# Ten slots instead of eight for the prepared expert weights of a decoder trunk, and two loads fewer ahead

## The chip, the cores and the metric

One core of a Trainium2 chip runs the whole program. The metric is the device time in microseconds. Before the change it is 1417.46 us, the median of three runs (1416.42 to 1417.75).

## The reference

Two decoder layers work on 256 tokens of 1024 features. Each mixes the tokens (a pooling group and a convolution group), norms, and then applies a channel mixer: layer 0 a dense SwiGLU, layer 1 the top 2 of 8 experts. Nearly all weights are the experts':

```python
def moe_swiglu(h, w_router, w1, w3, w2):
    ...
    for e in range(N_EXPERTS):
        out = out + gates[:, e:e + 1] * swiglu(t, w1[e], w3[e], w2[e])
```

w1 and w3 are 1024 x 3584, w2 is 3584 x 1024, all float32.

## The kernel before, in words

**Heads and rests.** TensorE multiplies in fp32r, which keeps fewer bits than float32. So each weight is split: ScalarE casts it to fp32r (the head, `nc.scalar.copy` in `Weights.advance`, L146) and VectorE subtracts the head from it (the rest, `Weights.rest`, L161). `mm` then issues three matmuls for each 128 rows of weights: activations' head by weights' head (L347), head by rest (L351), activations' rest by weights' head (L352). Where the activations' head and rest stand side by side in one tile, two do: L347 and L349.

**The experts.** The tokens of an expert are gathered into a tile of 128 places. Experts at even places of `SEQ` are *wide*: 128 places for tokens, three matmuls. Those at odd places are *narrow*: 64 places, heads beside rests, two matmuls, and a shift that folds the halves (L1052). An expert is cut into seven chunks of 512 hidden features. `BLOCKS` lists the 56 chunks: four wide ones first, then narrow and wide ones by turns, and four narrow ones last. Below, a *pair* is a narrow chunk with the wide one after it. `experts` runs over them: w1 of this chunk, w3 of this chunk, then w2 of the chunk before (`both`, `both`, `down`); SiLU is on ScalarE (L652), the gated product on VectorE (`glu`, L661), and `hidden` turns that product by four transposes on TensorE (L335) and splits it (L320 and L321, narrow: L381 and L382). Where the next expert is due, gather (L796) and scatter (L814, L815) lie in between.

**Items and slots.** Each chunk has six *items* of 128 x 2048 (1 MB): two of w1, two of w3, two of w2. All items lie in a pool of 19 slots of that size (`SLOTS`). An expert item takes three slots in its life: the loaded float32 one (SyncE, L117), a head and a rest. The loaded slot is free after the rest is made, head and rest after TensorE's last matmul on them. `get(i)` calls `advance`, which prepares items in order as long as those prepared and not yet used take at most `hl` slots, and keeps `ahead()` loads before the next item to prepare:

```python
            full = not it["direct"] and self.live(False) + it["slots"] > self.hl
...
        return max(1, SLOTS - self.temps - self.hl - self.live(True))
```

While the experts run, `hl` is `HL_MOE` (set in `moe` once the first chunk's w3 is done), and `temps` is 1, from the last seven chunks on 4. Engines run their instructions in the order in which they are emitted; a tile that finds no free slot waits for one to come free, so which slot it gets is settled when the program is built.

**Near the end** (`MORE_AT`, chunk 53) all engines read a count and branch (L1038, L1039).

Of the kernel before, what the change touches and what calls it, by code (L numbers as in the profile page):

```python
# [33 lines left out]
DENSE_CHUNKS = [(c * 512, min(512, DFF - c * 512)) for c in range((DFF + 511) // 512)]  # L34
ND = len(DENSE_CHUNKS)
SLOTS = 19
HL_START, HL_PRE, HL_FIRST, HL_SECOND, HL_MOE = 8, 12, 8, 6, 8
WO0 = 0
DIRECT = ("pw0", "pw1", "wo00", "wo01")
DT = ((20, 21), (20, 21))  # L40
# [1269 lines left out]
```

## Time and profile before

| what | value |
| --- | --- |
| median of three runs | 1417.46 us |
| the profiled execution's own time | 1417.34 us |
| its span | 1415.6 us |
| TensorE (PE) busy | 1310.6 us, 93% |
| VectorE (DVE) busy | 1199.9 us, 85% |
| ScalarE (ACT) busy | 938.9 us, 66% |
| moved by DMA | 433.07 MB, mean 306 GB/s |
| expert loads | 336 of 1 MB, median 8.0 us to landing |

The profile is that of one execution. Its span is 1.7 us shorter than its own time. The experts fill the stretch from about 490 to 1370 us. A matmul's duration there (some 0.39 us) includes its way through the array and overlaps with the next, so a busy TensorE is not one at its peak: what a wait costs is read from the distance of two starts.

### The profile page before, as it was taken

What the parts mean: (1) busy time and instruction counts of PE and PEld (TensorE: products, weight loads), DVE (VectorE), ACT (ScalarE), POOL (GpSimd) and SP (SyncE); (2) the same over time, 40 slices, a digit from 0 to 9 for tenths busy, and PEclk for the clock granted to TensorE, in tenths of its full rate; (3) what the DMA queues carried; (4) which work ended last, traced back from release to release, by engine and by line L of the source; (5) the groups of instructions that cost most, each with busy time, mean ns of one, the idle gap of its engine ahead of it and who ended that gap; (6) DMA issues with size and microseconds to landing.
All of it is one profiled execution on the core that took longest, in us unless ns stands there. A gap on an engine that the chain in (4) does not pass through costs nothing. (4 is left out here: it accounts for less than half of the span.)

```text
span 1415.6 us, 16882 instructions
## 1 busy us (share of the span) xinstructions
PE 1310.6 (93%) x6186; PEld 1060.0 (75%) x6186; DVE 1199.9 (85%) x1082; ACT 938.9 (66%) x883; POOL 92.3 (7%) x71
## 2 busy tenths in 40 slices
PE   6769999999869999999999999999999999999877
PEld 5638888888637887777777778778777777778656
DVE  3996844557966889999999999999999999999885
ACT  4543634426533668887887787787787788788662
POOL 0430000010560200000000000000000000000000
PEclk8889999999988999999999999999999999999999
DMA  9335755427544589999999999999999999999950
GB/s 381 121 119 178 266 180 179 178 97 272 196 173 177 204 334 406 420 387 350 418 417 354 402 420 353 391 417 367 384 421 376 375 409 387 371 360 423 356 191 30
DMA packets 62170, 433.07 MB, mean 306 GB/s; under 512 B 6960, under 2 KB 7472, under 8 KB 11008
## 3 DMA queue, kind: packets, MB, share of 16 engines
q1 hardware_dynamic: 60336, 425.60, 77.0%
q0 software_dynamic: 1168, 4.23, 0.9%
q10 hardware_dynamic: 576, 2.10, 0.5%
q8 instruction: 50, 0.82, 0.2%
q14 instruction: 40, 0.33, 0.1%
HBM read 430.85 MB, written 1.05 MB: 305 GB/s over the span
## 5 line engine op out<-in xcount | busy, mean ns | idle before, releaser
L161 DVE TENSOR_TENSOR w<-w 128x2048 fp32r<-128x2048 f32 (+1 forms) x460 | 895.9, 1988 | 72.6 <-ACT w L146 61.7
L146 ACT CAST w<-w 128x2048 fp32r<-128x2048 f32 (+1 forms) x460 | 751.1, 1671 | 157.1 <-PE p L351 39.5
L347 PE MATMUL p<-w,xH 128*128 128x512 f32 (+1 forms) x1096 | 434.5, 396 | 8.8 <-DVEq L1039 5.8
L352 PE MATMUL p<-w,xL 128*128 128x512 f32 (+1 forms) x648 | 251.0, 387 | 1.3 <-DVE xL L321 1.3
L351 PE MATMUL p<-w,xH 128*128 128x512 f32 (+1 forms) x648 | 250.3, 386 | 0.4 <-DVE w L161 0.4
L347 PEld LDWEIGHTS p<-w,xH 128*128 128x128 f32 x1096 | 207.8, 190 | 50.3 <-issue 6.5
L349 PE MATMUL p<-w,xH 128*128 128x512 f32 x448 | 180.3, 402 | 16.6 <-DVE w L161 16.6
L347 PE MATMUL y<-w,gH 128*128 128x512 f32 x448 | 176.4, 394 | 1.8 <-DVE gH L382 1.6
L352 PEld LDWEIGHTS p<-w,xL 128*128 128x128 f32 x648 | 122.5, 189 | 26.7 <-DVE xL L321 1.8
L351 PEld LDWEIGHTS p<-w,xH 128*128 128x128 f32 x648 | 122.7, 189 | 24.8 <-DVE w L161 1.3
L349 PEld LDWEIGHTS p<-w,xH 128*128 128x128 f32 x448 | 85.0, 190 | 46.8 <-DVE w L161 30.7
L347 PEld LDWEIGHTS y<-w,gH 128*128 128x128 f32 x448 | 84.6, 189 | 21.0 <-DVE gH L382 2.7
L490 DVE SCALAR_TENSOR_TENSOR yc<-w,vec,yc 128x256 f32<-128x256 f32 x156 | 91.8, 661 | 0.0
L349 PE MATMUL y<-w,gH 128*128 128x512 f32 x224 | 88.4, 395 | 2.4 <-DVE w L161 2.4
L351 PE MATMUL y<-w,gH 128*128 128x512 f32 x224 | 89.7, 400 | 0.0
L352 PE MATMUL y<-w,gL 128*128 128x512 f32 x224 | 87.4, 390 | 0.0
L498 POOL TENSOR_TENSOR gH<-gH,w 128x512 f32<-128x512 f32 x38 | 66.3, 1744 | 107.9 <-ACT w L495 105.5
L429 POOL DMA_DIRECT2D w<-in_pT x2 | 1.2, 580 | 984.6 <-DVE w L161 826.2
L652 ACT ACTIVATE s<-p 128x512 f32<-128x512 f32 (+1 forms) x69 | 41.0, 596 | 28.5 <-PE p L352 28.5
L321 DVE TENSOR_TENSOR gL<-tr,gH 128x512 fp32r<-128x512 f32 x38 | 25.6, 684 | 32.6 <-ACT gH L320 32.6
L351 PEld LDWEIGHTS y<-w,gH 128*128 128x128 f32 x224 | 42.0, 188 | 14.1 <-DVE w L161 6.0
L349 PEld LDWEIGHTS y<-w,gH 128*128 128x128 f32 x224 | 42.6, 190 | 11.7 <-DVE w L161 3.0
(223 smaller groups left out, 1454.2 us busy)
## 6 DMA issues: line engine op xcount, KB each, us to landing
w<-in_exp_w SPq DMA_DIRECT2D x336, 1024.0 KB, 8.0
w<-in_dense_w SPq DMA_DIRECT2D x33, 1024.0 KB, 5.1
w<-in_w_out SPq DMA_DIRECT2D x8, 1024.0 KB, 6.5
w<-in_ple_gate_w SPq DMA_DIRECT2D x8, 1024.0 KB, 5.3
w<-in_w_gv SPq DMA_DIRECT2D x6, 1024.0 KB, 6.1
w<-in_w_u SPq DMA_DIRECT2D x4, 1024.0 KB, 9.6
w<-in_w_gv SPq DMA_DIRECT2D x4, 512.0 KB, 6.9
w<-in_w_small SPq DMA_DIRECT2D x2, 1024.0 KB, 10.2
```

The lines of the kernel that those rows point to most:

```text
L146: nc.scalar.copy(h, w)
L161: engine.tensor_tensor(l, w, h.bitcast(F32), op=ALU.subtract)
L321: nc.vector.tensor_sub(dst.l, src, dst.h.bitcast(F32))
L347: nc.tensor.matmul(ps, x.h, wh, start=start, stop=False)
L349: nc.tensor.matmul(ps, x.h, wl, start=False, stop=stop)
L351: nc.tensor.matmul(ps, x.h, wl, start=False, stop=False)
L352: nc.tensor.matmul(ps, x.l, wh, start=False, stop=stop)
L429: nc.gpsimd.dma_start(pT.f, a["pT"][l])
L490: nc.vector.scalar_tensor_tensor(yc[:, ct], src, w1, yc[:, ct], op0=ALU.mult, op1=ALU.add)
L498: nc.gpsimd.tensor_tensor(part[b], part[b], p, op=ALU.add)
L652: nc.scalar.activation(s_[:, :nf], p1[:, :nf], AF.Silu)
```

## The change

`HL_MOE`, the number of slots for heads and rests while the experts run, goes from 8 to 10: five items instead of four. By `ahead()` the loads ahead go from 19 - 1 - 8 = 10 to 19 - 1 - 10 = 8, and in the last seven chunks (`temps` 4) from 7 to 5.

```diff
-HL_START, HL_PRE, HL_FIRST, HL_SECOND, HL_MOE = 8, 12, 8, 6, 8
+HL_START, HL_PRE, HL_FIRST, HL_SECOND, HL_MOE = 8, 12, 8, 6, 10
```

No instruction is added or taken away. VectorE's order, at the end of w3 of the second wide chunk and the w2 after it; `w_3151`, `w_3255`, `w_3263`, `w_3331`, `w_3333` and `w_3498` are loaded items in the order of their use, `g0` is the gated product, `gL0` the rest of its transposed form. Before:

```order
L161 TENSOR_TENSOR w_3617<-w_3151,w_3616 128x2048
L661 SCALAR_TENSOR_TENSOR g0_3632<-p3_3593,gsl0_3438,s0_3591 128x512
L161 TENSOR_TENSOR w_3637<-w_3255,w_3636 128x2048
L161 TENSOR_TENSOR w_3655<-w_3263,w_3654 128x2048
L321 TENSOR_TENSOR gL0_3671<-tr_3672,gH0_3670 128x512
L161 TENSOR_TENSOR w_3693<-w_3331,w_3692 128x2048
```

The same place with the change:

```order
L161 TENSOR_TENSOR w_3601<-w_3151,w_3600 128x2048
L161 TENSOR_TENSOR w_3619<-w_3255,w_3618 128x2048
L661 SCALAR_TENSOR_TENSOR g0_3634<-p3_3597,gsl0_3438,s0_3595 128x512
L161 TENSOR_TENSOR w_3639<-w_3263,w_3638 128x2048
L161 TENSOR_TENSOR w_3657<-w_3331,w_3656 128x2048
L321 TENSOR_TENSOR gL0_3673<-tr_3674,gH0_3672 128x512
```

The rest of `w_3255` now stands ahead of the gated product, and that of `w_3331` ahead of `gL0`: each rest is one item earlier against the work on activations. ScalarE's order a little further on, around the cast `gH0` of that transposed product. Before:

```order
L146 CAST w_3654<-w_3263 128x2048
L320 CAST gH0_3670<-tr_3672 128x512
L146 CAST w_3692<-w_3331 128x2048
L146 CAST w_3710<-w_3333 128x2048
L652 ACTIVATE s0_3726<-p1_3679 128x512
```

The same place with the change:

```order
L146 CAST w_3638<-w_3263 128x2048
L146 CAST w_3656<-w_3331 128x2048
L320 CAST gH0_3672<-tr_3674 128x512
L146 CAST w_3684<-w_3333 128x2048
L146 CAST w_3712<-w_3498 128x2048
L652 ACTIVATE s0_3728<-p1_3681 128x512
```

The cast of `w_3331` now stands ahead of `gH0` and that of `w_3498` ahead of SiLU: heads, too, are one item earlier. On SyncE the order of the loads stays; one load that stood ahead of the branch of L1039 now stands behind it.

The built programs also tell which earlier tile had a tile's slot. Of 280 expert items in the middle (the 31st load to the 310th), 263 take one slot of head or rest at least from an item three before, which TensorE must have used; with the change 258 take it from one four before. Of the loads, 187 take the slot of the load twelve before, once its rest is made; with the change 162 take that of the load ten before. (The others take a head's or a rest's slot.) So in the program as built, loads held more slots than `ahead()` counts and prepared items fewer than `hl` allows: three items, now four.

## Rows read from the trace of the kernel before

**Rows 1.** The page: slices of the span (DMA share, GB/s).
```profile
PEclk8889999999988999999999999999999999999999
DMA  9335755427544589999999999999999999999950
GB/s 381 121 119 178 266 180 179 178 97 272 196 173 177 204 334 406 420 387 350 418 417 354 402 420 353 391 417 367 384 421 376 375 409 387 371 360 423 356 191 30
```
**Rows 2.** Busy time of each engine in two stretches, experts and end.
```profile
core 0: us, PE busy (x) PEld busy (x) DVE busy (x) ACT busy (x) POOL busy (x), PEclk, DMA share, GB/s
560.00:1300.00 740.00, 715.72 (x3280) 576.59 (x3279) 704.89 (x462) 595.89 (x447) 0.00 (x0) 1.00 0.98 390
1300.00:1400.00 100.00, 80.75 (x327) 60.58 (x326) 86.30 (x76) 64.33 (x64) 4.51 (x5) 0.93 0.60 236
```
**Rows 3.** The same by pair of chunks, seven pairs (the pattern then repeats).
```profile
577.20:607.50 30.30, 29.61 (x132) 23.42 (x131) 29.20 (x18) 25.18 (x19) 0.00 (x0) 1.00 1.01 419
...
641.10:676.20 35.10, 33.38 (x150) 26.89 (x149) 32.58 (x24) 25.51 (x20) 0.00 (x0) 1.00 0.97 362
676.20:706.40 30.20, 29.51 (x132) 23.33 (x131) 29.13 (x18) 25.11 (x19) 0.00 (x0) 1.00 1.01 417
...
sum 225.90, PE 218.17 PEld 175.74 DVE 214.49 ACT 180.73 POOL 0.00; mean PE 31.17 PEld 25.11 DVE 30.64 ACT 25.82 POOL 0.00
```
**Rows 4.** Waits from 560 to 1300 us: total us, times, longest us.
```profile
ACT w L146 <- PE p L351: 34.2, 32, 1.7
...
DVE w L161 <- ACT w L146: 28.3, 59, 1.9
ACT w L146 <- PE y L347: 21.9, 16, 1.9
...
PE p L349 <- DVE w L161: 15.9, 20, 1.7
...
PE ps_xg L796 <- DVE cc L765: 3.5, 3, 1.2
PE tr L335 <- DVE g L661: 3.4, 3, 1.1
```
**Rows 5.** Timeline: w3 of a narrow chunk.
```profile
692.35 4.49 DVE L161 TENSOR_TENSOR w<-w 128x2048 fp32r<-128x2048 f32 x2
...
693.38 0.39 PE L349 MATMUL p<-w,xH 128*128 128x512 f32 x1
693.61 0.39 PE L347 MATMUL p<-w,xH 128*128 128x512 f32 x1
...
694.68 0.50 PE L349 MATMUL p<-w,xH 128*128 128x512 f32 x1 [0.69 <-DVE w L161]
```
**Rows 6.** Costly groups of VectorE and ScalarE, 577.2 to 803.1 us, each form apart.
```profile
L161 DVE TENSOR_TENSOR w<-w 128x2048 fp32r<-128x2048 f32 x85 | 191.7, 2288 | 11.8 <-ACT w L146 9.8 <-DMA w<-in_exp_w 0.9 <-PE y L351 0.4
L661 DVE SCALAR_TENSOR_TENSOR g<-p,gsl,s 128x512 f32<-128x512 f32 x15 | 11.2, 745 | 0.0
...
L146 ACT CAST w<-w 128x2048 fp32r<-128x2048 f32 x85 | 160.6, 1914 | 36.2 <-PE p L351 12.6 <-PE p L347 7.1 <-PE y L347 7.0
```
**Rows 7.** Expert loads issued by 703.9 us and their time to landing around it.
```profile
L117 SPq DMA_DIRECT2D w<-in_exp_w x102: 327/333/384, 363.4 to 703.8; - x102
...
DMA to landing us min/median/max: 6.9/8.4/9.7
```
**Rows 8.** Rests up to 706.3 us, casts up to 729.8 us.
```profile
L161 DVE TENSOR_TENSOR w<-w 128x2048 fp32r<-128x2048 f32 x85 | 192.9, 2299 | 15.0 <-ACT w L146 11.6 <-PE y L351 1.7 <-DMA w<-in_exp_w 0.9
...
L146 ACT CAST w<-w 128x2048 fp32r<-128x2048 f32 x96 | 181.4, 1914 | 42.1 <-PE p L351 15.1 <-PE p L347 6.9 <-PE y L351 6.8
```
**Rows 9.** The end: loads by 1303.9 us, landing there, casts up to 1321.4 us.
```profile
L117 SPq DMA_DIRECT2D w<-in_exp_w x325: 327/333/1278, 363.4 to 1303.7; - x163
...
DMA to landing us min/median/max: 7.0/9.6/11.5
...
L146 ACT CAST w<-w 128x2048 fp32r<-128x2048 f32 x319 | 601.8, 1914 | 124.9 <-PE p L351 38.7 <-PE y L347 23.4 <-PE y L351 22.7
```
**Rows 10.** Timeline: w2 of a narrow chunk, then the wide chunk's transposes.
```profile
713.84 0.39 PE L347 MATMUL y<-w,gH 128*128 128x512 f32 x1
...
716.82 0.74 DVE L661 SCALAR_TENSOR_TENSOR g<-p,gsl,s 128x512 f32<-128x512 f32 x1
...
717.62 0.66 PE L335 MATMUL tr<-con,g 128*128 128x128 f32 x4
```

## The prediction, made before the changed kernel ran

> **What bounds the kernel now.** I read the slices first, for the place of the experts [rows 1]; the reader is to see a DMA share of 9 tenths from the middle on, at 334 to 423 GB/s. Then the engines' busy time there [rows 2]: from 560 to 1300 us TensorE is busy for 715.7 of 740 us at a full clock, VectorE for 704.9, and the DMA share is 0.98. No engine is alone at its bound; each has 2 to 5% left, so a gain can only come from waits of one on another. By pairs of chunks [rows 3] the quickest take 30.2 to 30.3 us, those with a gather or a scatter 33 to 35, and seven pairs make the pattern of 225.9 us. VectorE idles for 225.9 - 214.5 = 11.4 us of them.
>
> Then the waits [rows 4]. TensorE waits 20 times, 15.9 us, for a rest, always at L349: the second matmul of a narrow item, whose head is there and whose rest is not. VectorE waits 59 times, 28.3 us, for a head, and ScalarE, before its casts, for TensorE (34.2 and 21.9 us are the two largest of such rows): it has the loaded item and no slot to put the head in. So the chain is a ring: TensorE frees slots, ScalarE casts, VectorE subtracts, TensorE uses the item. Last, the loads: 102 were issued by 703.9 us [rows 7]; six of them are the first chunk's, so the 102nd is the 96th cast, and that starts only at 729.8 us [rows 8]. Landing took 9.7 us at most there, so the item lay ready for some 16 us. Loads are early and slots for heads and rests are short.
>
> Why it happens in narrow chunks. TensorE's matmuls start 0.23 us apart (693.38 to 693.61) [rows 5]: a narrow item has 8 (1.8 us), a wide one 12 (2.7 us). A rest takes 2.29 us, two in a row 4.49 [rows 5, 6]. So VectorE falls behind by 0.4 us with each narrow item and could gain as much with each wide one, but there it stands waiting for heads, which wait for slots. What it fails to gain in the six wide items is missing in the six narrow ones.
>
> **The change, part by part.**
>
> *One more prepared item.* A head and rest had to wait for TensorE's end of the item three before, now of that four before (the slots of the built program, in the section on the change). Each becomes free to start one item's use earlier: 1.8 us by a narrow item, 2.7 by a wide one. What is it worth? One TensorE wait: the shown one has 694.68 - 693.61 = 1.07 us between two starts, less the usual 0.23, so 0.84 us lost where the row says 0.69; 0.15 us of each wait is hidden in the matmul's own duration [rows 5]. For 20 waits: 15.9 + 20 x 0.15 = 18.9 us [rows 4]. Can all of it go? An earlier start by 1.8 us or more covers 0.84, and the longest wait (1.7 + 0.15 = 1.85) about. But VectorE must find the time: in the pair of the shown wait it idles 30.20 - 29.13 = 1.07 us, more than 0.84; in the pair with the longest, 35.10 - 32.58 = 2.5 us, more than 1.85 [rows 3]. Of its idle time in seven pairs 9.8 us end with a head [rows 6], against some 18.9 x 225.9 / 740 = 5.8 us of TensorE's waits there. So all 18.9 us can go, with VectorE at 97 to 99% afterwards. **-18.9 us.**
>
> *Casts and rests ahead of the gated product.* One rest more stands ahead of `glu` on VectorE, and one cast more ahead of SiLU and of `gH0` on ScalarE. Behind the gated product TensorE's transposes wait: in the shown wide chunk w2 begins at 713.84, the product ends at 717.56, the transposes start at 717.62 [rows 10], so w2's 16 matmuls (3.6 us) just cover it. If VectorE has really run ahead, the extra rest was made in time that was idle before, and nothing is late. If it has not, the product is late by part of a rest, and TensorE stands. Bounds: below, nothing (or even the three waits that stand there now go, 3.4 + 3 x 0.15 = 3.9 us [rows 4]); above, a whole rest, 2.29 us, in each of the 740 / 32.3 = 23 wide chunks, 53 us. I take a value near the lower end, because VectorE's idle time of 9.8 us per seven pairs exceeds what it has to make up: as much again as the three waits of today. **+3.9 us.**
>
> *Two loads fewer ahead.* The load's slot now comes from the load ten before instead of twelve. Two items are 2 x 30.25 / 12 = 5 us, off a margin of 16 in the middle: nothing. At the end the margin is least: the 325th load is issued at 1303.7, is the 319th cast, and that starts at 1321.4; landing took at most 11.5 us, which leaves 6.2 us [rows 9]. Less 5 us about 1 us is left, and a shorter queue lands sooner, too. **0 us**, with a bound of +4: the margin's lack, paid once, since later loads come at the same pace. Below, nothing: an early load cannot gain. The one load now behind the branch would be needed some 15 us later there; no cost.
>
> The sum: -18.9 + 3.9 + 0 = -15.0 us. The profiled execution's own time is 1417.34 us, 0.12 below the median of the runs, so 1402.3 against it, and **1402.4 us** as a median.
>
> **A rule weighed.** At its best slice DMA moved 423 GB/s [rows 1], that is 2.48 us for 1.05 MB, 29.75 us for a pair's twelve. The quick pairs, at 30.2 us and a share of 1.01 [rows 3], can by that row shrink by 0.5 us and not by 0.84. But over seven pairs 84 loads take 208 us of 225.9, and the margin of 16 - 5 = 11 us lends what two quick pairs in a row lack, so the sum keeps the full term.
> The Trainium skill (DMA: Bandwidth & Descriptors, Specifications) gives 358 GB/s as the limit of one core's share of HBM and 435 as that of the fabric. The trace disagrees with the first as a bound here (423 in a slice); by it twelve loads would take 35.1 us and no pair could become quicker, so the sum would be 0. By the second they take 28.9 us (an estimate from that page), and the sum would stay at -15.0.
>
> **The rivals.**
>
> *Loads become the bound.* Each quick pair stops at 29.75 us. For: a share of 1.01 in them. Against: the margin. Three of seven pairs are quick, 10 in 740 us; each keeps 0.84 - 0.5 = 0.34 us of its loss: 3.4 us. Time: 1402.4 + 3.4 = 1406. It lies inside the range.
>
> *The wait only moves.* TensorE no longer waits at L349, but at the transposes for the gated product; or the slots gained by heads and rests do not let VectorE run ahead, because ScalarE, in order, sits at another wait. For: VectorE is busy for 29.1 of 30.2 us in quick pairs already. Against: 59 waits of VectorE for heads. Time: -3 to +2 us, 1414.5 to 1419.5, say 1417. This is also what comes if the program does not do what the change says.
>
> *Slower: the gated product late in every wide chunk.* If cast and rest of the item ahead of it both start only after TensorE's w3, the product ends 1.91 + 2.29 + 0.75 = 4.95 us after it [rows 6], and w2's 16 narrow matmuls cover 3.6: 1.3 us lost, which is just what the three waits of today show (3.9 / 3). In all 23 wide chunks that is 30 us, less the 3.9 there now and the 18.9 gained: +7, 1425 us. It decides from 18 such chunks on. Against: three in 740 us have it now, though three items are ahead and not four.
>
> **How the numbers follow.** Forecast, with the load-bound rival inside it: 0.82, 1392 to 1413. The wait only moves: 0.11, 1413 to 1420. Late product: 0.07, 1420 and above. The lower end of the forecast takes all 18.9 us and the waits at the transposes and at the gather (L765: 3.5 + 0.45) with them: 1417.46 - 18.9 - 3.9 - 3.9 = 1391; I end at 1393. The upper keeps half of the waits and adds the product's and the loads' bound partly: -9.5 + 3.9 + 2 = -3.6, 1413.8; I end at 1413. What lies outside 1393 to 1413 are the two other rivals and a little of the forecast's own ends, 2 in 10. A measurement of this kernel tells about 0.2%, 2.8 us, from no change: faster means under 1414.6, slower over 1420.3. Faster 0.83, same 0.10, slower 0.07.
>
> **What would show it.** Right: from 560 us on, the row of TensorE's waits at L349 falls from 20 to a few; VectorE's waits for heads fall from 28.3 us to under 12; the quick pairs come to 29.3 to 29.8 us; VectorE is busy for 97% or more and GB/s rises from 390 to near 400; the time from load to cast shrinks by 5 us and ScalarE has no new wait for a load. Wrong: the waits at L335 for the gated product grow past 10 us, the pairs stay at 30.2, or after 1290 us casts wait for loads.

## The result and the profile after

The changed kernel takes **1395.68 us** (median of four runs, 1394.91 to 1396.02) against 1417.28 us (1416.42 to 1417.75) of the kernel before on the same chip: a ratio of 0.9842, 95% interval 0.983 to 0.9854. That is 21.6 us faster; forecast were 15.0, with a range of 1393 to 1413. The profiled execution's own time is 1394.91 us, its span 1393.1 us.

The page's slices, which answer to [rows 1]:

```profile
PEclk8889999999989899999999999999999999999998
DMA  9334755526545399999999999999999999999850
GB/s 381 129 112 166 264 187 196 192 69 242 219 167 187 109 363 364 421 421 376 403 420 408 400 421 387 390 421 405 400 421 404 376 420 414 388 378 420 353 211 30
```

The two stages by engine [rows 2]:

```profile
560.00:1300.00 740.00, 728.01 (x3384) 599.23 (x3383) 724.48 (x476) 618.89 (x468) 0.62 (x1) 1.00 1.00 405
1300.00:1400.00 100.00, 71.78 (x306) 56.57 (x304) 65.85 (x70) 42.15 (x48) 3.90 (x4) 0.88 0.41 159
```

In the same 740 us TensorE starts 3384 matmuls instead of 3280, VectorE is busy for 724.5 us instead of 704.9, and loads move 405 GB/s instead of 390. The same seven pairs of chunks as in [rows 3], cut where the same rests end:

```profile
576.60:605.50 28.90, 28.90 (x132) 23.66 (x131) 28.89 (x18) 24.95 (x18) 0.00 (x0) 1.00 1.01 420
...
638.00:672.80 34.80, 34.77 (x158) 28.56 (x157) 32.47 (x24) 27.14 (x22) 0.00 (x0) 1.00 0.97 365
672.80:701.50 28.70, 28.25 (x129) 22.83 (x127) 28.70 (x18) 24.77 (x18) 0.00 (x0) 1.00 1.01 422
...
sum 217.40, PE 214.17 PEld 176.44 DVE 212.53 ACT 180.25 POOL 0.00; mean PE 30.60 PEld 25.21 DVE 30.36 ACT 25.75 POOL 0.00
```

The quick pairs fell from 30.2 to 28.7 and 28.9 us, the seven from 225.9 to 217.4. VectorE's idle time in them went from 11.4 to 4.9 us. The waits from 560 to 1300 us [rows 4] tell why:

```profile
ACT w L146 <- PE p L351: 38.1, 37, 1.7
...
DVE w L161 <- ACT w L146: 13.3, 13, 1.9
...
PEld tr L335 <- DVE g L661: 12.7, 17, 1.6
...
PE tr L335 <- DVE g L661: 5.6, 7, 1.1
...
PE ps_xg L796 <- DVE cc L765: 3.5, 3, 1.2
```

The row of TensorE's waits at L349 is gone: 20 waits, 15.9 us before, none now. VectorE's waits for heads fell from 59 to 13. The waits for the gated product went from 3 to 7.

Where does the gain arise? TensorE's transposes of the gated product of the 49th expert chunk, before and after:

```profile
1256.30 0.60 PE L335 MATMUL tr<-con,g 128*128 128x128 f32 x4
```
```profile
1233.76 0.60 PE L335 MATMUL tr<-con,g 128*128 128x128 f32 x4
```

They start 22.5 us earlier, and the span is 22.5 us shorter: the gain is made up to there and kept. (Rests seem to gain more, the 289th of a whole item 24.8 us, since with the change they run one item further ahead of TensorE. So progress is compared here by TensorE's instructions, not by rests.)

### The profile page after: what moved, and what is told of

Read it like the earlier page. It is cut to its first block, busy times and chain, and to the rows that moved or that the text cites. A ratio compares the mean times of both kernels' runs of the same rounds, so it can differ in the third digit from the quotient of the medians.

```text
span 1393.1 us, 16896 instructions
## 1 busy us (share of the span) xinstructions
PE 1302.4 (93%) x6186; PEld 1067.9 (77%) x6186; DVE 1194.2 (86%) x1082; ACT 936.8 (67%) x883; POOL 92.1 (7%) x71
## 5 line engine op out<-in xcount | busy, mean ns | idle before, releaser
L349 PE MATMUL p<-w,xH 128*128 128x512 f32 x448 | 176.1, 393 | 0.0
L347 PEld LDWEIGHTS y<-w,gH 128*128 128x128 f32 x448 | 84.6, 189 | 21.4 <-DVE gH L382 3.0
L349 PEld LDWEIGHTS p<-w,xH 128*128 128x128 f32 x448 | 85.1, 190 | 17.0
L349 PE MATMUL y<-w,gH 128*128 128x512 f32 x224 | 88.3, 394 | 1.9 <-DVE w L161 1.9
L320 ACT CAST gH<-tr 128x512 fp32r<-128x512 f32 x38 | 21.8, 586 | 43.6 <-PE tr L335 43.0
L349 PEld LDWEIGHTS y<-w,gH 128*128 128x128 f32 x224 | 42.5, 190 | 11.0 <-DVE w L161 2.3
```

The costliest lines, as they stand in the source:

```text
L320: nc.scalar.copy(dst.h, src)
L347: nc.tensor.matmul(ps, x.h, wh, start=start, stop=False)
L349: nc.tensor.matmul(ps, x.h, wl, start=False, stop=stop)
```

## The experiments

**Each part of the change alone.** The theory: slots that waiting loads held do the work once heads and rests have them, not the count `HL_MOE` as such. The rival: the count, which lets preparation run further ahead, does it. Two loads fewer, with the old count:

```diff
-HL_START, HL_PRE, HL_FIRST, HL_SECOND, HL_MOE = 8, 12, 8, 6, 10
+HL_START, HL_PRE, HL_FIRST, HL_SECOND, HL_MOE = 8, 12, 8, 6, 8
...
-        return max(1, SLOTS - self.temps - self.hl - self.live(True))
+        return max(1, SLOTS - self.temps - self.hl - self.live(True) - 2 * self.fewer)
```

(`fewer` is 1 while the experts run.)

> HL_MOE stays 8 (four items counted, casts and rests at their old places in ScalarE's and VectorE's order), but two loads fewer are kept ahead. In the built program loads then hold ten to eleven slots and heads and rests take those of four items before. Theory (slots that loads gave up are the gain): nearly the whole gain, 1394 to 1400 us, no waits of TensorE at L349 for a rest between 560 and 1270 us, and fewer than today's seven waits for the gated product, since it stands one rest earlier. Rival (the count of prepared items, that is the order, is the gain): 1415 to 1420 us, twenty waits at L349 as before.

Measured: 1395.17 us, ratio 0.9835 (0.9814 to 0.9855), as with the whole change. In its program 267 of 280 items take a slot from four items before. Its waits from 560 to 1270 us (its lines are one higher than the change's):

```profile
DVE w L162 <- ACT w L147: 13.9, 29, 1.3
PEld p L350 <- DVE w L162: 8.3, 20, 0.9
PEld y L352 <- DVE w L162: 5.8, 20, 0.3
PE p L350 <- DVE w L162: 1.6, 3, 0.5
```

No wait for a gated product is left here; three small ones for a rest are. So the two loads fewer alone give the whole gain.

Then the count alone, with ten loads ahead as before:

```diff
-        return max(1, SLOTS - self.temps - self.hl - self.live(True))
+        return max(1, SLOTS - self.temps - self.hl - self.live(True) + 2 * self.fewer)
```

> HL_MOE 10 as in the change, but ten loads are kept ahead as before, on the same 19 slots. In the built program loads hold twelve to thirteen slots and 183 of 280 items take a slot of three before. Theory (slots): no gain or a loss, 1412 to 1425 us, the waits at L349 still there, and more waits for the gated product than in the changed kernel. Rival (order): 1394 to 1400 us.

Measured: 1435.09 us, ratio 1.0134 (1.0112 to 1.0156): 17.9 us slower than the kernel before. In its program 183 of 280 items still take a slot from three items before. Its busy time and waits from 560 to 1270 us:

```profile
560.00:1270.00 710.00, 668.76 (x3088) 542.99 (x3087) 665.11 (x437) 560.76 (x421) 0.00 (x0) 1.00 0.98 384
```
```profile
ACT w L147 <- DVE w L162: 45.6, 84, 1.4
DVE w L162 <- ACT w L147: 34.7, 65, 1.7
PE tr L336 <- DVE g L662: 28.7, 28, 1.4
```

This is the mechanism of the slower rival of the prediction: the gated product is late 28 times, 28.7 us, for up to 1.4 us each (the rival's price was 1.3). It is late in most wide chunks, as the rival had it, and in most narrow ones as well, which the rival left out. The rest that was put ahead of it waits for its head, the head for a slot, and the product behind them in VectorE's order waits, too.

**More and fewer items.** Twelve slots and six loads ahead, by the table alone (`HL_MOE` 12):

> HL_MOE 12: six items counted, six loads ahead, five items before in the built program, loads on the slot of eight before. Theory: nothing left to gain in the middle (no rest waits are left), so the pairs from 576 to 1230 us stay within 0.3 us; near the end the margin from landing to cast, 0.7 us in the changed kernel, goes below zero, casts wait for loads after some 1250 us and cost 2 to 8 us: 1397 to 1404 us. Rival (depth still limits): 1385 to 1393 us.

Measured: 1397.55 us, ratio 0.9871 (0.9847 to 0.9895). The theory held: TensorE begins the transposes of the 49th chunk at 1233.7 us, as with the change, so the middle gains nothing, and the span is 2.5 us longer; at the end a cast starts the moment its load lands (margin 0.0 us). And six slots with twelve loads ahead (`HL_MOE` 6):

> HL_MOE 6: three items counted, twelve loads ahead; in the built program 240 of 280 items take a slot of two before, most heads that of a load, so a rest (2.29 us) starts at the end of the item two before and TensorE has one item to cover it. Theory (slots): a narrow item covers 1.8 us, 0.5 us short, and the gated product, behind such a rest, comes late as well: 3 to 5 us a pair, 1480 to 1540 us. Rival (the loads ahead are worth as much as the slots): 1417 us or less, since loads lie ready earlier than ever.

Measured: 1451.15 us, ratio 1.0227 (1.0201 to 1.0253). The direction held, the size was too high, and no transposes wait for a late gated product here, against the theory. In the program 240 of 280 items take a slot from two before, and the waits at L349, which the change took away, grow (560 to 1270 us):

```profile
PEld p L349 <- DVE w L161: 56.8, 73, 2.3
ACT w L146 <- DVE w L161: 53.3, 108, 1.1
DVE w L161 <- ACT w L146: 34.4, 45, 1.4
PE p L349 <- DVE w L161: 24.3, 35, 1.9
```

Twelve slots in the middle and fewer at the end would be better, if the end alone spoiled them: `HL_MOE` 12, and from the last seven chunks on 8 with two loads fewer than the count allows (five).

```diff
-                W.temps = TEMPS_END
+                W.temps, W.hl, W.fewer = TEMPS_END, 8, 1
```

> Six items counted (12 slots) until the last seven chunks, then four, with five loads ahead: the middle of the run with HL_MOE 12 and an end like that of the run with fewer loads alone. Theory: the middle's end (rest of the 289th item) at about 1228 us as with 12, the end without casts that wait for loads: 1391 to 1395 us, a little under the changed kernel. Rival (the depth at the end matters too): 1396 to 1400 us.

Measured: 1396.71 us, ratio 0.9855 (0.9838 to 0.9871). The rival was right. The margin at the end is 2.6 us, and still nothing is gained: from the first expert chunk's transposes to those of the 49th chunk it takes 753.6 us, as with twelve slots throughout, and from there to the end of the span 161.7, where the change takes 159.4. What delays the end is not shown.

**What binds after the change.** VectorE is busy for 97.9% and TensorE for 98.4% of the stage. The change without the in-loop additions of the scattered expert outputs (`tensor_add` in `scatter`, left out in 28 instructions, so the output lacks them):

```diff
-                nc.vector.tensor_add(yo, yo, ps)
+                if add:
+                    nc.vector.tensor_add(yo, yo, ps)
```

> The changed kernel without VectorE's 28 additions of the scattered results (L817) of the first seven experts; the additions are left out, the matmuls before them stay. 28 x 0.61 us = 17 us less for VectorE. Theory A (VectorE, busy for 98% of the stretch, is the bound now): 1378 to 1384 us. Theory B (TensorE at its pace, or the loads at 2.48 us each, bound it as much): a third of it or less, 1390 to 1396 us.

And the change with a quarter of one rest in six made twice:

```diff
+                    if self.made in self.twice:
+                        self.rest(nc.vector, l[:, :512], w[:, :512], h[:, :512])
```

> The changed kernel with a quarter of one rest in six made twice on VectorE (the first w2 item of 55 chunks, 512 columns, the same values again): 55 x 0.58 us = 32 us more. Theory A: the whole of it, 1424 to 1430 us. Theory B (there is slack beside it): 1400 to 1415 us.

Measured: 1386.16 us without the additions (ratio 0.9788, 0.9769 to 0.9807), 1418.15 us with the doubled quarters (1.0006, 0.9996 to 1.0015). The busy time of the first, then of the second:

```profile
560.00:1250.00 690.00, 683.04 (x3188) 563.81 (x3187) 665.48 (x425) 577.04 (x437) 0.00 (x0) 1.00 1.00 406
```
```profile
560.00:1300.00 740.00, 713.09 (x3295) 581.30 (x3294) 731.28 (x509) 601.16 (x449) 0.00 (x0) 1.00 0.98 393
```

Some 19 us less of VectorE's work (28 x 677 ns) give 9.5 us, but between the first and the 49th chunk, where 24 of the 28 additions stood, only 4.3; some 38 us more (55 x 692 ns) cost 22.5, 20.3 of them there. Both times lie between the theories: work that is added counts for some 0.6 of itself, work that is taken away for half or less. In the first run VectorE has idle time (665.5 of 690) and TensorE little (683.0), so the amount of VectorE's work is not all that holds the changed kernel.

**Work taken off VectorE.** One rest in twelve goes to GpSimd, on top of the twelve-slot version (1396.71 us):

```diff
+    for e, c in BLOCKS[:-WIDE_FIRST]:
+        if e % 2:
+            W.slow.add(W.names[f"w2e{e}_{c}"][0])
```

> The kernel above with one rest in twelve (the first w2 item of 24 narrow chunks, used after four wide items) on GpSimd, idle so far. 24 x 2.24 = 54 us less for VectorE. Theory A without contention: a rest of 128x2048 takes some 7 us on GpSimd by the 1.74 us of 128x512 there, ready in time five items ahead: VectorE no longer bounds, loads at 2.48 us do: 1365 to 1380 us. Rival (both engines read SBUF through one port and block each other): 24 x up to 7 us lost on VectorE, 1400 to 1540 us.

Measured: 1424.22 us, ratio 1.0045 (1.0028 to 1.0062), 27.5 us slower than without it. The timeline of one such rest, and VectorE's groups from 560 to 1300 us:

```profile
707.95 5.00 POOL L162 TENSOR_TENSOR w<-w 128x2048 fp32r<-128x2048 f32 x1 [25.23 <-ACT w L147]
...
710.88 4.24 DVE L162 TENSOR_TENSOR w<-w 128x2048 fp32r<-128x2048 f32 x1 [1.73 <-ACT w L147]
```
```profile
L162 DVE TENSOR_TENSOR w<-w 128x2048 fp32r<-128x2048 f32 x254 | 601.8, 2416 | 43.1 <-ACT w L147 35.2 <-POOL w L162 4.4 <-issue 2.4
...
L772 DVE TENSOR_SCALAR m<-con,cc 128x128 f32<-128x128 f32 x12 | 14.0, 1165 | 0.0
```

The rest on VectorE that overlaps it takes 4.24 us: it ends at 715.12, which is GpSimd's end (712.95) plus 2.17, about a whole rest. So it is held until GpSimd is through. The Trainium skill (SBUF — State Buffer, SBUF: two separate sides) says that GpSimd and an instruction of VectorE with two SBUF inputs share a pair of ports, which one of them holds for its whole length. The trace agrees with that for these rests. What it costs shows at TensorE: from 560 to 1270 us it waits 13 times, 15.0 us, for the gated product, which VectorE makes between its rests; without rests on GpSimd it did so 3 times, 1.2 us.

**Fewer loads still.** Since the loads' slots did the work, how few loads are enough? Count 10 as in the change, and three loads ahead until the last seven chunks:

```diff
-        return max(1, SLOTS - self.temps - self.hl - self.live(True))
+        return max(1, SLOTS - self.temps - self.hl - self.live(True) - 5 * self.fewer)
```

> HL_MOE 10 with three loads ahead instead of eight until the last seven chunks; the slots stand there unused or go to heads and rests, which take those of six before; loads take those of eight before (slots) or six. Theory: the margin from landing to cast, 11 us in the middle of the changed kernel, shrinks by 2 to 4 items of 2.6 us, to 1 to 6 us, and the loads' 2.48 us each begin to hold the quick pairs (28.7 us in the changed kernel) near 29.8: 1398 to 1410 us. Rival (loads have room left): 1393 to 1397 us.

Measured: 1392.35 us, ratio 0.9806 (0.9781 to 0.9832). My theory was wrong; the rival was nearer, and the time is below even its bounds. The median time from landing to cast is 0.4 us (10.9 in the change), and ScalarE waits for loads; but TensorE has no wait for a rest (560 to 1270 us):

```profile
ACT w L147 <- DMA w<-in_exp_w: 40.0, 76, 2.0
...
PE ps_xg L797 <- DVE cc L766: 4.5, 3, 2.1
PEld tr L336 <- DVE g L662: 2.6, 6, 0.6
```

The slots come from six items back, so a cast that is late by up to 2.0 us is made up before TensorE wants its item. Then five loads ahead (`- 3 * self.fewer`), with the one of three and the change once more on the same chip:

> Five loads ahead instead of eight until the last seven chunks, everything else as changed. By the theory that any slot taken from loads that wait helps as long as TensorE finds its item, the heads and rests come from about five to six items before, the landing-to-cast margin falls to some 4 us in the middle, and the time lies between the change's 1395.7 and the 1392.4 of three loads ahead: 1391 to 1396. Rival: past four items nothing more is gained and the 3 us between the change and three loads ahead are what different jobs differ by; then all three kernels of this job lie within 2 us of each other.

> Three loads ahead until the last seven chunks, beside the change itself on one chip. If a shorter queue of loads is truly better, it is 2 to 4 us under the change again; by the rival, within 2 us of it.

> The change itself once more, for the comparison on one chip: 1394.5 to 1396.5.

Measured, with 1418.1 us for the kernel before: five loads **1383.29 us** (1382.68 to 1384.87), ratio 0.9761 (0.9745 to 0.9777); three loads 1391.51, ratio 0.9818 (0.9802 to 0.9834); the change 1395.03, ratio 0.9836 (0.9819 to 0.9852). The last two came as expected; the first lies some 8 us below the lower end of what the theory gave. Five loads ahead beat both kernels: 34.8 us under the one before, 11.7 under the change. Its pairs, and its waits from 560 to 1300 us:

```profile
573.90:602.60 28.70, 28.70 (x131) 23.70 (x131) 28.70 (x17) 24.89 (x19) 0.00 (x0) 1.00 1.02 421
602.60:633.30 30.70, 30.45 (x156) 25.59 (x155) 30.70 (x26) 24.55 (x20) 0.00 (x0) 1.00 1.01 420
...
sum 214.70, PE 213.97 PEld 177.44 DVE 211.79 ACT 178.43 POOL 0.00; mean PE 30.57 PEld 25.35 DVE 30.26 ACT 25.49 POOL 0.00
```
```profile
ACT gH L382 <- PE tr L336: 37.8, 23, 2.7
...
DVE w L162 <- ACT w L147: 7.6, 6, 1.3
...
PE ps_xg L797 <- DVE cc L766: 1.2, 3, 0.5
...
PE tr L336 <- DVE g L662: 0.7, 1, 0.7
```

TensorE is busy for 214.0 of 214.7 us; until 1200 us it waits for no rest and no gated product, and ScalarE now waits for TensorE's transposes. That is what the change left on the table: its seven pairs take 217.4, with TensorE waiting for the gated product. The next bound is TensorE's own work, as the table below shows.

**What the series says together.** Two numbers describe each kernel: how many items the order of instructions runs ahead (`HL_MOE` / 2), and how many items back the slot of a head or rest was last used (read from the built program). Two more are read from the traces: the time between the transposes of the first and of the 49th expert chunk, and what TensorE loses in it (of each distance of two starts over 0.25 us, all beyond the usual 0.23).

| order ahead | loads ahead | slots from | us | 1st to 49th chunk | of it lost | what is late |
| --- | --- | --- | --- | --- | --- | --- |
| 3 | 12 | 2 before | 1451.2 | 805.6 | 71.0 | rests |
| 4 | 10 | 3 before | 1417.3 | 776.3 | 41.8 | rests (kernel before) |
| 5 | 10 | 3 before | 1435.1 | 792.2 | 58.2 | gated product |
| 4 | 8 | 4 before | 1395.2 | 749.0 | 15.6 | rests, by little |
| 5 | 8 | 4 before | 1395.7 | 752.8 | 19.9 | gated product, by little (the change) |
| 6 | 6 | 5 before | 1397.6 | 753.6 | 20.5 | gated product, by little; loads at the end |
| 5 | 5 | 5 before | 1383.3 | 742.4 | 10.4 | no rest, no product until 1200 us |
| 5 | 3 | 6 before | 1392.4, 1391.5 | 748.5, 747.0 | 15.6, 14.1 | loads |

Without what is lost, each of these kernels takes 732 to 735 us for the stretch: that is TensorE's own work, and the eight differ by how long TensorE waits. More slots help until loads are late. An order that runs further ahead than the slots brings nothing (1395.2 and 1395.7) or does harm (1417.3 and 1435.1), since the product stands behind a rest that waits. The rows of 5 and 6 ahead with slots from 5 before fit that (1383.3 and 1397.6): in their programs loads, too, mostly take the slot of the same load, eight before. But they also differ in the loads ahead, and the order by itself at five slots was not tried.

## Why the prediction was right, and where its sum was off

**The ring was the bound, and rests were what TensorE missed: right.** The row at L349 fell from 20 to none, VectorE's waits for heads from 28.3 to 13.3 us (forecast: under 12, a little too much), VectorE's share came to 97.9% and GB/s to 405. The two parts run alone show that it is the slots: 1395.17 with the loads' slots alone.

**The term of -18.9 us: right for what it counted, and too small for what it stood for.** The distances of all TensorE starts, from 546 us to the same matmul (1240 us before, 1217 after), hold 38.9 us over the usual ones before and 17.1 after. Of the difference of 21.8 us, 17.7 are the 18 waits for a rest in that stretch, at 0.65 to some 1.9 each, twelve of them at the 0.84 that the prediction read. Another 5.9 are small delays of 0.1 us that no row of TensorE's waits names. In the timeline of before, at the wait of [rows 5] and at the w2 item behind it:

```profile
694.79 0.19 PEld L347 LDWEIGHTS p<-w,xH 128*128 128x128 f32 x1
695.02 0.40 PE L347 MATMUL p<-w,xH 128*128 128x512 f32 x1
...
696.88 0.19 PEld L351 LDWEIGHTS y<-w,gH 128*128 128x128 f32 x1 [0.30 <-DVE w L161]
696.88 0.50 PE L351 MATMUL y<-w,gH 128*128 128x512 f32 x1
...
697.22 0.39 PE L352 MATMUL y<-w,gL 128*128 128x512 f32 x1
```

The matmul behind the wait starts 0.34 us after 694.68, not 0.23: 0.10 more per wait. And at 696.88 only the weight load waited, 0.30 us; TensorE has no wait there, but the next start is 0.34 off as well. Such waits have rows of their own, under PEld, which I had passed over, because a weight load overlaps matmuls. Before the change, 560 to 1300 us:

```profile
PEld p L349 <- DVE w L161: 29.0, 33, 2.1
...
PEld tr L335 <- DVE g L661: 8.3, 12, 1.6
PEld y L351 <- DVE w L161: 5.8, 20, 0.3
```

The first and the last are gone with the change. A sum that counts a start's whole delay and the next one's would have had 5.9 us more.

**The term of +3.9 us for the gated product: half of it, +1.9.** Waits for it went from 3 to 7 rows, 5.6 us, under the 10 that were to be a sign of error. By starts, 5.3 us became 7.1. The place of [rows 10] with the change:

```profile
713.56 0.74 DVE L661 SCALAR_TENSOR_TENSOR g<-p,gsl,s 128x512 f32<-128x512 f32 x1
...
713.99 0.39 PE L349 MATMUL y<-w,gH 128*128 128x512 f32 x1
714.33 2.29 DVE L161 TENSOR_TENSOR w<-w 128x2048 fp32r<-128x2048 f32 x1
714.36 0.42 PEld L335 LDWEIGHTS tr<-con,g 128*128 128x128 f32 x4 [0.41 <-DVE g L661]
714.36 0.65 PE L335 MATMUL tr<-con,g 128*128 128x128 f32 x4
```

The product ends at 714.30, the transposes start 0.06 us later, as before the change; only their weight load waited, and 0.37 us lie between the last two starts where 0.23 are usual: 0.14 lost. The extra rest stands ahead of the product nearly for free, because VectorE makes it in time that was idle before, as argued. The rival that prices a late product in every wide chunk was not wrong about its mechanism: with the count alone it came, 28 times in wide and narrow chunks.

Together: -18.9 - 5.9 + 1.9 = -22.9, against 1417.34 - 1394.91 = 22.4 us between the two profiled executions. The three terms are read from stretches of different length, so that they agree to half a microsecond is in part luck. So is the place of 1395.7 us in the range: the prediction's lower end took the waits at the transposes and at the gather to go as well. They stayed (5.6 and 3.5 us); what brought the time down there were the small delays, which the sum did not have.

**The 0 us for the loads: right, with the margin forecast.** At the end the smallest time from landing to cast is 0.7 us (landed 1297.7, cast 1298.4) where about 1 was forecast. In the middle the median is 10.9 us after 18.2 before, so the margin shrank by 7.3 us where the sum took 5, and a shorter queue did not land sooner: the median landing of an expert load went from 8.0 to 8.8 us. There was room for both; from 560 to 1300 us ScalarE has no row of waits for a load. That the whole gain would come from the loads' slots, and that still fewer loads would be a gain beyond it, I had not seen.

**Quick pairs under 29.3 us: missed to the good side.** They came to 28.7 and 28.9, at 420 to 422 GB/s, below the 29.75 us that the best slice gave as the loads' floor. The loads lent what was missing, as the sum had it. In such a pair neither engine has idle time left: TensorE is busy for 28.90 and VectorE for 28.89 of 28.90 us. The rival *loads become the bound* is refuted by this, *the wait only moves* by the seven pairs.

## What to carry to other kernels

Where loads and prepared tiles share one pool, compare the time that a loaded tile lies ready (16 us here) with the time by which the consumer's tile is late (0.8 us): a slot belongs where it is missed, and the built program tells which tile truly gets it. Let the order run only as far ahead as there are slots, or else the tile that waits for one holds up whatever stands behind it. And price a wait by the distance of starts over the whole stretch, weight-load rows included, not by its row alone.

## What the runs showed of the hardware that I had not expected

With three 1 MB loads ahead, which land 0.4 us (median) before their cast, DMA still moves 409 GB/s from 560 to 1270 us; with eight ahead it moved 404, with ten 389. Three ahead take some 8 us more than five (1391.5 and 1383.3); that the late loads are the cause of all of it is not shown, since the slots differ as well.

A rest of 128 x 2048 takes GpSimd 5.09 us and VectorE 2.28; with GpSimd at work, VectorE's own took up to 6.33 us, and a 128 x 128 instruction (L772 there) 1.17 us in the mean instead of 0.29. Moving 24 rests, some 55 us of VectorE's work, made the kernel 27.5 us slower.
